# Attention: other engines for the sum of two output halves and for the scaling of probabilities

## The chip, the cores and the metric

The kernel runs on one core of a Trainium2 chip. Its metric is the device time of one execution in microseconds; lower is better. The core has a matrix engine (TensorE, in the profile PE, with its weight loads as PEld), two engines for element-wise work that can read the matrix engine's result memory PSUM (VectorE, DVE, and ScalarE, ACT), a third one without access to PSUM (GpSimd, POOL), and DMA queues (SP is one of the engines that start them). Each engine carries out its own instructions in order; between engines, semaphores order them.

## The reference, cut to what matters

Two layers of a decoder trunk: 512 tokens, 1024 features. Each layer mixes tokens in three parallel ways (sparse attention, gated linear attention, spatial gating), projects their joined outputs back, and adds a SwiGLU block. The change lies in the sparse attention, 8 heads of 64 in two groups that share keys and values. Each head has three branches, whose outputs are weighted by gates and added:

```python
s = jnp.einsum('bqghd,bcgd->bghqc', qb, kc)          # compressed keys
p_cmp = masked_softmax(s, ...)
o_cmp = jnp.einsum('bghqc,bcgd->bqghd', p_cmp, vc)
...                                                  # selected and window keys alike:
p = masked_softmax(s, tok <= t[None, None, None, :, None])
o_slc = jnp.einsum('bghqm,bgqmd->bqghd', p, vsel)
...
return gb[..., 0:1] * o_cmp + gb[..., 1:2] * o_slc + gb[..., 2:3] * o_win
```

With 512 tokens, 8 blocks of 64 and a window of 512, the selected and the window branch both become causal attention over all earlier tokens, with keys and values of their own.

## The kernel before, in words

Products run in float32 with a rounded high part and a remainder: every operand is split into `hi` (a copy into the type that TensorE rounds to) and `lo` (operand minus `hi`), and three products are added (`mm3`, L335). `split_psum` (L298) is that split: ScalarE copies `hi`, VectorE subtracts `lo`.

The attention (L1188 to L1290) goes over four pairs of heads `hp`, in each over two heads `hh`, in each over two branches `br`, in each over four tiles `i` of 128 query tokens. Tile `i` sees 128 x (i + 1) keys, so the probability tiles are 128, 256, 384 and 512 columns wide. Per branch:

- Scores: two matmuls into a bank of ring `s` (three banks), the negated row maximum on VectorE (L1218, L1237), the exponential with its row sum on ScalarE (L1222, L1239). The two narrow tiles of both branches are made together in the first branch.
- `rr`, four columns: reciprocal of the row sums and multiplication by the gate, both on VectorE (L1244, L1245).
- Scaling of the four probability tiles in place by their columns of `rr` (L1247 to L1253). `ISP` and `ISA` (L54, L55) say which tile goes where: tile 3 (512 columns) to GpSimd (L1249), tile 2 (384) to ScalarE (L1251), tiles 0 and 1 (128 and 256) to VectorE (L1253). A dependency written by hand (L1255) makes GpSimd's scaling wait for VectorE's last one.
- Transposes on TensorE (L1262) in three groups: key block 0 of all four query tiles, key block 1 of three, blocks 2 and 3 together. Each group is split by `split_psum` into `pt` (in the profile PT), and two matmuls per block, with `hi` (L1275) and `lo` (L1276), add it to the head's output bank `O`. Ring `o` has one bank only, so the next head's first L1275 needs it free.

At the head's end the compressed branch is added (L1286, L1287). `O` then holds the output in two halves, from the high and the low part of v, on different partitions. They are added into a half of `oc`, a tile of a ring of six (`tmp`): ScalarE copies one half (L1288), VectorE adds the other from PSUM (L1289). After both heads of a pair `split_psum` makes the two parts of the output projection's operand, `kt` (L1290).

Nothing here writes down the order of the engines' queues. A planner sorts the instructions by priority (program order, with offsets for some) and by its own estimate of when each is ready. So products of the output projection's first half, `out_proj(l, okt, 4, ...)` (L1673), which need nothing of the attention, lie among the attention's matmuls as fillers (L336 to L338), and so do the residual additions that go with them (L500). The queries of later heads are moved into place by GpSimd (`load_q`, L1186).

Of the kernel before, what the change touches and what calls it, by code (L numbers as in the profile page):

```python
# [10 lines left out]
F32 = mybir.dt.float32  # L11
# [5 lines left out]
ALU = mybir.AluOpType  # L17
AX = mybir.AxisListType

P = 128  # L20
# [7 lines left out]
H = 8  # L28
# [22 lines left out]
PREP = {(0, 0): (("q", 0), ("q", 1)), (0, 1): (("c", 0),), (0, 3): (("d", 0),), (1, 0): (("q", 2),), (2, 0): (("q", 3),), (2, 3): (("c", 1),),  # L51
        (4, 0): (("d", 1),)}
NBOTH = 2
ISP = (3,)  # L54
ISA = (2,)  # L55
PBK = {"g": 2, "s": 3, "t": 2, "o": 1}
JG = ((0,), (1,), (2, 3))
BTAGS = "ggsssgto"
# [85 lines left out]
def trunk_kernel(ctx: ExitStack, tc: tile.TileContext, a, out):  # L144
    nc = tc.nc
# [9 lines left out]
    def nm(s):  # L155
        uid[0] += 1
        return f"{s}_{uid[0]}"
# [7 lines left out]
    def psum(tag):  # L165
        taken[tag] += 1
        return banks[:, rings[tag][(taken[tag] - 1) % len(rings[tag])], :]

    def small(n, tag, bufs=4, dt=F32):
        return sm.tile([P, n], dt, tag=tag, name=nm(tag), bufs=bufs)  # L170
# [127 lines left out]
    def split_psum(hi, lo, src):  # L298
        nc.scalar.copy(hi, src)  # L299
        nc.vector.tensor_tensor(lo, src, hi.bitcast(F32), op=ALU.subtract)  # L300
# [88 lines left out]
    with tc.tile_pool(name="x0", bufs=1, reuse_waits="tile") as xp:  # L389
# [22 lines left out]
        def e_load(q, k0):  # L412
# [9 lines left out]
                          reason="first loads alone")  # L422
# [144 lines left out]
    def mixer(l, norm, xkt, eu=None):  # L567
# [65 lines left out]
        with tc.tile_pool(name=f"mx{l}", bufs=1, reuse_waits="tile") as mp:  # L633
            def tmp(n=SEQ, dt=F32):
                return mp.tile([P, SEQ], dt, tag="tmp", name=nm("tmp"), bufs=6)[:, 0:n]
# [11 lines left out]
            with tc.tile_pool(name=f"ma{l}", bufs=1, reuse_waits="tile") as ap:  # L647
# [29 lines left out]
                for lp in range(2):  # L677
                    hs = slice(64 * lp, 64 * lp + 64)
# [4 lines left out]
                for w_i in range(2):  # L683
                    pa = pos_t(w_i, l).rearrange("p (s a) -> p a s", s=2)
                    for s in range(2):
                        hi, lo = (kvR[w_i][:, :, 65 * s : 65 * s + 1, h] for h in range(2))
# [374 lines left out]
            with tc.tile_pool(name=f"mt{l}", bufs=1, reuse_waits="tile") as tp_:  # L1061
# [20 lines left out]
                for g in range(G):  # L1082
                    for b in range(2):
                        prep_k(g, b)
                    hi = km2[g][64:128].rearrange("p b (n c) -> p b n c", c=P)
# [99 lines left out]
                def load_q(h):  # L1185
                    (nc.gpsimd.tensor_copy if h > 1 else nc.scalar.copy)(qm1[h % GH][0:64], qst[h // GH][0:64, h % GH, :])  # L1186

                for hp in range(H // 2):  # L1188
                    if hp % 2 == 0:
                        okt[hp // 2] = kt_tile()  # L1190
                    kt = okt[hp // 2]
                    oc = tmp()
                    for hh in range(2):
                        h = 2 * hp + hh
                        g, h4 = h // GH, h % GH
# [5 lines left out]
                        O = psum(OT[h % len(OT)])  # L1201
                        first = True
                        for br in range(2):
# [23 lines left out]
                            ps_ = [pb[br] for pb in both]  # L1227
# [15 lines left out]
                            rr = small(NT, "rr", 4)  # L1243
                            nc.vector.reciprocal(rr, den)  # L1244
                            nc.vector.tensor_tensor(rr, rr, gates[:, :, 3 * h + 1 + br], op=ALU.mult)  # L1245
                            scaled = None
                            for i in SORD:  # L1247
                                if i in ISP:
                                    p3 = nc.gpsimd.tensor_tensor(ps_[i], ps_[i], rr[:, i : i + 1].to_broadcast([P, P * (i + 1)]), op=ALU.mult)  # L1249
                                elif i in ISA:  # L1250
                                    nc.scalar.activation(ps_[i], ps_[i], AF.Copy, scale=rr[:, i : i + 1])  # L1251
                                else:
                                    scaled = nc.vector.tensor_scalar(ps_[i], ps_[i], rr[:, i : i + 1], None, op0=ALU.mult)  # L1253

                            tc.add_manual_dep(p3.ins, scaled.ins.name, mybir.DependencyInfo(mybir.DependencyClass.Sync, mybir.DependencyReason.DATA),  # L1255
                                              reason="port")
                            for js in JG:
                                T = psum(TT[js[0]])
                                c = 0
# [24 lines left out]
                        hs = slice(64 * hh, 64 * hh + 64)  # L1284
# [1 line left out]
                        nc.tensor.matmul(O, lhs, pcT[g][0], start=False, stop=False)  # L1286
                        nc.tensor.matmul(O, lhs, pcT[g][1], start=False, stop=True)  # L1287
                        nc.scalar.copy(oc[hs, :], O[ls, :])  # L1288
                        nc.vector.tensor_tensor(oc[hs, :], oc[hs, :], O[hs, :], op=ALU.add)  # L1289
                    split_psum(kt[:, hp % 2, 0, :], kt[:, hp % 2, 1, :], oc)  # L1290
            return okt

    def out_proj(l, okt, k0, kts, nrm, tags=None):
# [375 lines left out]
    for l in range(L):  # L1669
        okt = mixer(l, norm, xkt, eu if l == 0 else None)  # L1670
        fnorm = Norm()
        with tc.tile_pool(name=f"ff{l}", bufs=1, reuse_waits="tile") as fp:
            out_proj(l, okt, 4, None, None)  # L1673
            fkt = [kt_tile() for _ in range(4)]
            out_proj(l, okt, 0, fkt, fnorm, BTAGS)
            ops = Ops(g_ffn(l), fkt, fp)
            if l < L - 1:
                norm = Norm()
                xkt = []
                ffn(l, fp, fnorm, fkt, ops, xkt, norm, g_attn(l + 1))  # L1680
            else:
                ffn(l, fp, fnorm, fkt, ops, None, None, None)
# [24 lines left out]
```

## Time and profile before

| | |
|---|---|
| median of 3 runs | 1287.74 us (1286.69 to 1287.77) |
| profiled execution | 1286.52 us, its span 1284.7 us, granted clock 0.997 |
| attention, layer 0 | some 183 to 282 us of the span |
| attention, layer 1 | some 814 to 912 us of the span |
| scalings on GpSimd (L1249) | 32, of 1.04 us each |
| second halves added by VectorE (L1289) | 16, of 0.68 to 0.69 us each |

How to read it: a line of a group gives the code line, the engine, the operation, output and inputs by the program's names with their shapes, the count, then busy time and the mean of one in ns, then the engine's idle time before them and what ended it. A line of a timeline gives start and duration in us, engine, line and operation, and in brackets the idle time before it and its releaser. Waits name who waited, for whom, the total, the count and the longest.

### The profile page before, as it was taken

The page shows a single profiled execution, that of the slowest core. Times are in us where ns is not written, and L with a number is a line of the kernel's source. Part 1 is how long each engine was busy: PE and PEld are TensorE (multiplying, and loading weights), DVE is VectorE, ACT ScalarE, POOL GpSimd, SP SyncE. Part 2 cuts the span into 40 slices and gives each one's busy share as a digit, 9 for nine tenths or more (in the row PEclk, how much of TensorE's full clock was granted, in tenths as well). Part 3 has the DMA queues.
Part 4 walks back from the last instruction along what each step waited for, and adds up shares of the span by engine and source line. Part 5 has one row for each costly group of instructions (what it writes and reads, how often), then busy time and mean ns, then how long its engine had stood idle before and what let it go on. Part 6 is the DMA issues. An engine that isn't in the chain of part 4 may idle for free. (4 is left out here: it accounts for less than half of the span.)

```text
span 1284.7 us, 18046 instructions
## 1 busy us (share of the span) xinstructions
PE 1257.3 (98%) x6678; PEld 1038.5 (81%) x6678; DVE 918.2 (71%) x1645; ACT 677.0 (53%) x1288; POOL 160.5 (12%) x157
## 2 busy tenths in 40 slices
PE   8999999999999999999999999999999999999997
PEld 7888788778888888888888877777788888888886
DVE  6767799977856775587446678998767457827775
ACT  6675367864533553354346733788544445515532
POOL 0101222122000100010301012121210001000102
PEclk9999999999999999999999999999999999999999
DMA  6451441034335885483434317210533448754811
GB/s 231 142 180 34 115 108 33 17 87 127 98 105 141 197 232 146 111 200 99 115 94 149 116 34 175 64 33 3 146 98 99 131 117 210 216 130 133 227 66 66
DMA packets 134204, 155.01 MB, mean 121 GB/s; under 512 B 9307, under 2 KB 86885, under 8 KB 134117
## 3 DMA queue, kind: packets, MB, share of 16 engines
q1 hardware_dynamic: 117392, 128.81, 33.3%
q0 software_dynamic: 10208, 20.84, 9.2%
q10 hardware_dynamic: 6516, 4.22, 1.5%
q8 instruction: 52, 0.85, 0.3%
q14 instruction: 36, 0.29, 0.1%
HBM read 149.92 MB, written 2.10 MB: 118 GB/s over the span
## 5 line engine op out<-in xcount | busy, mean ns | idle before, releaser
L318 ACT CAST hl<-raw 128x1024 fp32r<-128x1024 f32 (+3 forms) x170 | 175.2, 1035 | 226.5 <-PE banks L338 160.9
L321 DVE TENSOR_TENSOR hl<-raw,hl 128x1024 fp32r<-128x1024 f32 (+3 forms) x170 | 207.1, 1222 | 94.6 <-ACT hl L318 93.0
L336 PE MATMUL banks<-hl,kt 128*128 128x512 f32 (+2 forms) x688 | 257.9, 375 | 1.1 <-ACT hl L318 1.1
L337 PE MATMUL banks<-hl,kt 128*128 128x512 f32 (+2 forms) x688 | 256.4, 373 | 0.0
L338 PE MATMUL banks<-hl,kt 128*128 128x512 f32 (+2 forms) x688 | 256.1, 373 | 0.0
L337 PE MATMUL banks<-kt,hl 128*128 128x512 f32 x384 | 151.5, 394 | 0.0
L338 PE MATMUL banks<-kt,hl 128*128 128x512 f32 x384 | 151.1, 394 | 0.0
L336 PE MATMUL banks<-kt,hl 128*128 128x512 f32 x384 | 150.4, 394 | 0.0
L336 PEld LDWEIGHTS banks<-hl,kt 128*128 128x128 f32 x688 | 129.5, 188 | 23.6 <-ACT hl L318 1.9
L337 PEld LDWEIGHTS banks<-hl,kt 128*128 128x128 f32 x688 | 129.5, 188 | 21.8 <-DVE hl L321 0.3
L338 PEld LDWEIGHTS banks<-hl,kt 128*128 128x128 f32 x688 | 129.4, 188 | 21.7
L318 ACT CAST hl<-wx 128x1024 fp32r<-128x1024 f32 x48 | 50.5, 1052 | 79.8 <-PE banks L338 69.1
L337 PEld LDWEIGHTS banks<-kt,hl 128*128 128x128 f32 x384 | 72.2, 188 | 14.7 <-DVE kt L295 0.9
L338 PEld LDWEIGHTS banks<-kt,hl 128*128 128x128 f32 x384 | 72.3, 188 | 13.7
L336 PEld LDWEIGHTS banks<-kt,hl 128*128 128x128 f32 x384 | 72.0, 188 | 13.3 <-ACT kt L299 0.3
L321 DVE TENSOR_TENSOR hl<-wx,hl 128x1024 fp32r<-128x1024 f32 x48 | 58.7, 1224 | 18.4 <-ACT hl L318 18.2
L500 DVE TENSOR_TENSOR xT<-xT,banks 128x512 f32<-128x512 f32 x56 | 37.5, 681 | 47.6 <-PE banks L338 47.6
L337 PE MATMUL banks<-act,hl 128*128 128x512 f32 x172 | 67.0, 390 | 0.0
L338 PE MATMUL banks<-act,hl 128*128 128x512 f32 x172 | 66.9, 389 | 0.0
L336 PE MATMUL banks<-act,hl 128*128 128x512 f32 x172 | 66.9, 390 | 0.0
L300 DVE TENSOR_TENSOR PT<-banks,PT 128x384 fp32r<-128x384 f32 (+1 forms) x96 | 54.6, 597 | 14.1 <-ACT PT L299 13.2
L336 PE MATMUL banks<-hl,act 128*128 128x512 f32 (+1 forms) x164 | 63.0, 384 | 0.0
(356 smaller groups left out, 2404.1 us busy)
## 6 DMA issues: line engine op xcount, KB each, us to landing
raw<-in_w_gate_dram SPq DMA_DIRECT2D x44, 512.0 KB, 3.9
raw<-in_w_up_dram SPq DMA_DIRECT2D x44, 512.0 KB, 4.0
raw<-in_w_in_dram SPq DMA_DIRECT2D x32, 512.0 KB, 3.7
raw<-in_w_down_dram SPq DMA_DIRECT2D x36, 256.0 KB, 4.0
raw<-in_w_down_dram SPq DMA_DIRECT2D x18, 512.0 KB, 3.7
raw<-in_w_out_dram SPq DMA_DIRECT2D x16, 512.0 KB, 4.3
raw<-in_cmp_w_k_dram SPq DMA_DIRECT2D x8, 512.0 KB, 3.9
raw<-in_cmp_w_v_dram SPq DMA_DIRECT2D x8, 512.0 KB, 4.9
```

Source lines behind the costliest of these rows:

```text
L300: nc.vector.tensor_tensor(lo, src, hi.bitcast(F32), op=ALU.subtract)
L318: last_cast[:] = [nc.scalar.copy(hl[:, 0, 0:n], raw[:, 0:n])]
L321: e_.tensor_tensor(hl[:, 1, 0:n], raw[:, 0:n], hl[:, 0, 0:n].bitcast(F32), op=ALU.subtract)
L336: nc.tensor.matmul(ps, lh, rh, start=start, stop=False, skip_group_check=skip)
L337: nc.tensor.matmul(ps, lh, rl, start=False, stop=False, skip_group_check=skip)
L338: return nc.tensor.matmul(ps, ll, rh, start=False, stop=stop, skip_group_check=skip)
L500: nc.vector.tensor_tensor(xT[:, m, :], xT[:, m, :], ps, op=ALU.add)
```

## The change

Three things change. Tile 2 of the probabilities (384 columns) is scaled by GpSimd too, tile 1 (256) by ScalarE, and only tile 0 (128) by VectorE; both GpSimd scalings wait for VectorE's one. In the first three pairs of a layer the second half of a head's output is copied by ScalarE into a tile of its own, `od`, instead of being added by VectorE. For these pairs a `join` adds the halves and makes the operand's low part on GpSimd, with ScalarE's copy for the high part in between; it stands in the program behind the scaling of the next pair's first branch. The fourth pair is treated as before.

```diff
-ISP = (3,)
-ISA = (2,)
+ISP = (2, 3)
+ISA = (1,)
...
+                joins = []
+
+                def join(hi, lo, oc, od):
+                    nc.gpsimd.tensor_tensor(oc, oc, od, op=ALU.add)
+                    nc.scalar.copy(hi, oc)
+                    nc.gpsimd.tensor_tensor(lo, oc, hi.bitcast(F32), op=ALU.subtract)
+
...
                     oc = tmp()
+                    od = tmp() if hp < H // 2 - 1 else oc
...
-                            scaled = None
+                            scaled, p3s = None, []
                             for i in SORD:
                                 if i in ISP:
-                                    p3 = nc.gpsimd.tensor_tensor(ps_[i], ps_[i], rr[:, i : i + 1].to_broadcast([P, P * (i + 1)]), op=ALU.mult)
+                                    p3s.append(nc.gpsimd.tensor_tensor(ps_[i], ps_[i], rr[:, i : i + 1].to_broadcast([P, P * (i + 1)]), op=ALU.mult))
...
-                            tc.add_manual_dep(p3.ins, scaled.ins.name, mybir.DependencyInfo(mybir.DependencyClass.Sync, mybir.DependencyReason.DATA),
-                                              reason="port")
+                            for p3 in p3s:
+                                tc.add_manual_dep(p3.ins, scaled.ins.name, mybir.DependencyInfo(mybir.DependencyClass.Sync, mybir.DependencyReason.DATA),
+                                                  reason="port")
+                            if joins:
+                                join(*joins.pop())
...
                         nc.scalar.copy(oc[hs, :], O[ls, :])
-                        nc.vector.tensor_tensor(oc[hs, :], oc[hs, :], O[hs, :], op=ALU.add)
-                    split_psum(kt[:, hp % 2, 0, :], kt[:, hp % 2, 1, :], oc)
+                        if od is oc:
+                            nc.vector.tensor_tensor(oc[hs, :], oc[hs, :], O[hs, :], op=ALU.add)
+                        else:
+                            nc.scalar.copy(od[hs, :], O[hs, :])
+                    if od is oc:
+                        split_psum(kt[:, hp % 2, 0, :], kt[:, hp % 2, 1, :], oc)
+                    else:
+                        joins.append((kt[:, hp % 2, 0, :], kt[:, hp % 2, 1, :], oc, od))
```

## The prediction

> **What bounds the kernel now.** I read the page first, then the table by stage, then the waits of TensorE's weight loads, which show what each loaded column block had to wait for.
>
> ```profile
> span 1284.7 us, 18046 instructions
> ...
> PE 1257.3 (98%) x6678; PEld 1038.5 (81%) x6678; DVE 918.2 (71%) x1645; ACT 677.0 (53%) x1288; POOL 160.5 (12%) x157
> ```
>
> TensorE has work in 98% of the span. No other engine can be worth more than the moments in which TensorE stands still, so the question is how many of these lie in the stage that the change touches. The table by stage has, per row, the stretch, its length, and the busy time with the number of instructions for PE, PEld, DVE, ACT and POOL. The two rows are the first and the second half of layer 0's attention.
>
> ```profile
> 183.00:232.00 49.00, 47.03 (x269) 38.13 (x268) 46.16 (x107) 38.62 (x106) 10.74 (x12) 1.00 0.09 28
> 232.00:282.00 50.00, 46.62 (x259) 35.82 (x257) 39.83 (x91) 36.37 (x101) 10.76 (x10) 1.00 0.26 63
> ```
>
> In the first half VectorE is busy 46.16 of 49 us, ScalarE 38.62, GpSimd (POOL) 10.74. TensorE still reaches 47.03, since the planner fills its gaps with products of the output projection. In the second half TensorE loses 3.4 us. So the stage is short of VectorE time and has much POOL time left. The waits of layer 0 (175 to 290 us; who waited for whom, total us, times, longest):
>
> ```profile
> PEld banks L1275 <- ACT PT L299: 7.6, 18, 1.2
> PEld banks L1276 <- DVE PT L300: 3.7, 10, 0.9
> PEld banks L1262 <- POOL P L1249: 2.6, 6, 0.8
> ```
> ```profile
> PE banks L1275 <- DVE tmp L1289: 0.8, 1, 0.8
> ```
>
> Three links of one chain stop TensorE: POOL's scaling holds the transposes (L1262), ScalarE's high part of the transposed probabilities (PT) holds the first product with v, VectorE's low part the second. The evacuation of the head's output bank (L1289) does so once. Layer 1 is the same chain again, so I price one layer and double it.
>
> **The change part by part.** The durations, from one profiled execution (count, then busy time and mean ns; for the lines asked for alone, min/median/max ns):
>
> ```profile
> L1239 ACT ACTIVATE P<-banks,nmx 128x512 f32<-128x512 f32 x16 | 11.2, 700 | 3.0 <-DVE nmx L1237 3.0
> L1251 ACT ACTIVATE P<-P,rr 128x384 f32<-128x384 f32 x16 | 10.0, 624 | 4.1 <-DVE rr L1245 4.1
> ...
> L1239 ACT ACTIVATE P<-banks,nmx 128x384 f32<-128x384 f32 x16 | 9.4, 589 | 2.3 <-PE banks L1262 1.7 <-DVE nmx L1237 0.3 <-DVE PT L300 0.2
> ...
> L1288 ACT COPY tmp<-banks 64x512 f32<-64x512 f32 x8 | 4.7, 581 | 3.4 <-PE banks L1287 3.3
> ...
> L299 ACT CAST kt<-tmp 128x512 fp32r<-128x512 f32 x4 | 2.5, 625 | 0.8 <-DVE tmp L1289 0.8
> ```
> ```profile
> L1253 DVE TENSOR_SCALAR P<-P,rr 128x256 f32<-128x256 f32 x16 | 5.6, 347 | 0.0
> L1289 DVE TENSOR_TENSOR tmp<-tmp,banks 64x512 f32<-64x512 f32 x8 | 5.5, 684 | 3.3 <-ACT tmp L1288 3.0
> ...
> L1253 DVE TENSOR_SCALAR P<-P,rr 128x128 f32<-128x128 f32 x16 | 4.5, 279 | 0.1
> L1245 DVE TENSOR_TENSOR rr<-rr,gates 128x4 f32<-128x4 f32 x16 | 4.3, 268 | 0.1
> ...
> L300 DVE TENSOR_TENSOR kt<-tmp,kt 128x512 fp32r<-128x512 f32 x4 | 2.8, 688 | 0.7 <-ACT kt L299 0.7
> ```
> ```profile
> L1249 POOL TENSOR_TENSOR P<-P,rr x32: 1039/1040/1043, 183.3 to 902.0; 128x512 f32<-128x512 f32 x32
> ```
> ```profile
> L1383 POOL TENSOR_TENSOR yg<-zb,gf x6: 1281/1292/1297, 1252.7 to 1270.3; 128x512 f32<-128x512 f32 x6
> ```
> ```profile
> L905 POOL TENSOR_TENSOR kr<-tmp,tmp x8: 721/736/1050, 124.5 to 776.0; 128x256 f32<-128x256 f32 x8
> ```
>
> *Work per layer.* VectorE loses 16 scalings of 256 columns (16 x 0.347 = 5.6), the additions of six heads (6 x 0.684 = 4.1) and the low parts of three pairs (3 x 0.688 = 2.1): 11.8 us, none added. ScalarE scales 256 instead of 384 columns; 128 columns are worth 0.700 - 0.589 = 0.11, so 0.51 for 0.62, 16 x 0.11 = 1.8 less; six second copies of an output half add 6 x 0.58 = 3.5; net +1.7. The three copies of the pair's high part (0.625) stay, at a later place. POOL gets 16 scalings of 384 columns and three joins. The 384 is not in the trace: its bounds are the 0.72 of a 256 addition and the 1.04 of 512. Additions of two full tiles cost 1.28 at 512 and 0.72 at 256, 2.2 ns a column; the 512 scaling with its repeated factor costs 1.04, so I scale 1.28 - 128 x 0.0022 = 1.00 by 1.04/1.28 and take 0.81, nearer to the 512 row, which is the same instruction. A join is two operations on two full 512 tiles, 2 x 1.28 = 2.6. POOL gains 16 x 0.81 + 3 x 2.6 = 20.8 us a layer and would stand at about 42 of 99: no bound by its sum, only by its delays.
>
> *The POOL link.* POOL starts after VectorE's last scaling and now has two in a row. Head 7 of layer 0:
>
> ```profile
> 269.10 0.55 DVE L1253 TENSOR_SCALAR P<-P,rr 128x128 f32<-128x128 f32 x2
> ...
> 269.81 1.04 POOL L1249 TENSOR_TENSOR P<-P,rr 128x512 f32<-128x512 f32 x1 [7.55 <-ACT P L1239]
> 269.98 0.89 DVE L1245 TENSOR_TENSOR rr<-rr,gates 128x4 f32<-128x4 f32 x1
> ...
> 270.91 0.66 PE L1262 MATMUL banks<-ident,P 128*128 128x128 f32 x4 [0.20 <-POOL P L1249]
> ...
> 270.97 0.61 ACT L1251 ACTIVATE P<-P,rr 128x384 f32<-128x384 f32 x1 [1.23 <-DVE rr L1245]
> ```
>
> The two VectorE scalings took 0.55 together, the first 0.28, so POOL may start 0.26 earlier; its 0.81 more makes the 512 tile ready 0.55 later, and TensorE's transpose, which today starts 0.06 after POOL's end (269.81 + 1.04 = 270.85, then 270.91), moves with it. Six of a layer's sixteen scalings stop TensorE (the wait row above). They are of two kinds; head 4 shows the other:
>
> ```profile
> 240.36 0.68 DVE L300 TENSOR_TENSOR kt<-tmp,kt 128x512 fp32r<-128x512 f32 x1
> 240.96 0.28 DVE L1253 TENSOR_SCALAR P<-P,rr 128x128 f32<-128x128 f32 x1
> 241.29 0.56 DVE L300 TENSOR_TENSOR PT<-banks,PT 128x384 fp32r<-128x384 f32 x1
> 241.76 0.34 DVE L1253 TENSOR_SCALAR P<-P,rr 128x256 f32<-128x256 f32 x1
> ```
> ```profile
> 242.27 1.04 POOL L1249 TENSOR_TENSOR P<-P,rr 128x512 f32<-128x512 f32 x1 [5.53 <-DVE P L1253]
> ```
>
> Here something lay between the two scalings, so dropping the second pays for the 384 by itself (241.24 + 0.17 + 0.81 + 1.04 = 243.26 against 243.31; 0.17 is the time from VectorE's end to POOL's start here). Besides, the pair's low part at 240.36 goes away and the chain starts 0.6 sooner. Counting three of each kind: 3 x 0.55 = +1.65 and -0.6 per layer. The other ten scalings end before TensorE asks; what hides their delay is earlier work in TensorE's queue.
>
> *What waits behind POOL.* The multiplication of four columns, all 32 of it:
>
> ```profile
> L1245 DVE TENSOR_TENSOR rr<-rr,gates x32: 93/160/892, 181.9 to 900.4; 128x4 f32<-128x4 f32 x32
> ```
>
> At 269.98 it took 0.89 instead of the median's 0.16, and ended with POOL's instruction; the mean of 268 ns above says that it isn't alone. ScalarE, which runs in order, then waited 1.23 for it. With POOL occupied for 1.85 instead of 1.04 this lasts up to 0.81 longer, at some four heads a layer; mostly the same moment as the late transpose, so I add 0.5 a layer (bounds 0 and 4 x 0.81 = 3.2).
>
> [...]
>
> *The output bank.* Today ScalarE copies one half and VectorE adds the other. Head 5 (VectorE, then ScalarE):
>
> ```profile
> 261.09 0.69 DVE L1289 TENSOR_TENSOR tmp<-tmp,banks 64x512 f32<-64x512 f32 x1
> 261.81 1.16 DVE L300 TENSOR_TENSOR PT<-banks,PT 128x512 fp32r<-128x512 f32 x2
> ```
> ```profile
> 260.92 0.97 ACT L299 CAST PT<-banks 128x512 fp32r<-128x512 f32 x2
> ```
>
> The addition ends at 261.78 and the low part follows at once. Two ScalarE copies in a row instead push the high part back by about 0.5 (0.58 less the overlap of two neighbours), while the low part need not queue: +0.2 and -0.4 per layer. In heads 0 to 3 fillers cover either; heads 6 and 7 keep the addition.
>
> *The joins.* Those of heads 2 and 4 fit into POOL's idle time (5.53 above). Head 6's doesn't:
>
> ```profile
> 261.23 1.04 POOL L1249 TENSOR_TENSOR P<-P,rr 128x512 f32<-128x512 f32 x1 [0.78 <-PE banks L1262]
> ```
> ```profile
> 263.46 0.71 PE L1262 MATMUL banks<-ident,P 128*128 128x128 f32 x5
> ```
>
> POOL is idle for 0.78 between the head's two branches, and the second branch's widest tile is needed at about 263.9, 1.6 after its end at 262.27. A first join operation (1.28) just fits ahead of the second branch; if the other half gets in between too, 1.0 is lost. I take half: +0.5 (bounds 0 and 1.0).
>
> *The sum.* 1.65 - 0.6 + 0.5 + 0.2 - 0.4 + 0.5 = +1.85 a layer, +3.7 in all. From the profiled execution's 1286.5 that is 1290.2; the median of the runs (1287.74) stands 1.2 above that execution, so 1291.4.
>
> **The rivals.**
> *VectorE's relief decides (faster).* VectorE was busy 86.0 of these 99 us and loses 11.8. If half of the waits for low parts (1.9), the wait for the output bank (0.8) and, through earlier maxima and exponentials, a third of the waits for high parts (2.5) go, 5.2 a layer are won against costs of 1.65 + 0.5 + 0.2 = 2.35: -2.85 a layer, 1286.5 - 5.7 + 1.2 = 1282.0; without the costs 1277.3. For it speaks the first half's 46.16 of 49. Against it: the largest wait is ScalarE's, which gets more work, and on head 7's path the removed pieces lie only just ahead of POOL. It decides if the planner, with less VectorE work, leaves fillers over for the second half.
> *Nothing shows.* The planner lays the order anew from its own estimates; it can put a filler or the next head's scores where POOL is late. Gains and losses of 1 to 2 us a layer then cancel: 1287.7.
> *POOL in VectorE's way.* If each of four multiplications waits the whole 0.81 and head 6's join costs its 1.0, the layer's sum is 1.85 - 0.5 + 3.2 + 0.5 = 5.05: 1286.5 + 10.1 + 1.2 = 1297.8. It decides once POOL passes from one instruction to the next without letting VectorE in.
>
> **How the numbers follow.** About 0.2% (2.6 us) is what a measurement of this kernel can tell from no change. The forecast, 1291.4, gets 0.34; POOL in VectorE's way 0.09; nothing shows 0.22; VectorE's relief 0.35. So faster 0.35, same 0.22, slower 0.43. Both signs hold much of the chance, so the range spans them, from 1279.5, between the relief's two prices, to 1297.0, just short of the collision's; the forecast's own range goes from 1288.9, the lower bounds of its terms (3 x 0.46 with the 384 at 0.72, then -0.6 + 0.2 - 0.4), to 1294.6, half of the way to the collision.
>
> **What would show it.** Right: the last transposes of heads 5 to 7 start about 0.5 later after VectorE's first scaling and end their idle time on POOL more often than six times a layer; the four-column multiplication's mean goes above 268 ns; ScalarE's busy time in these stretches stays near 75 us while VectorE's falls from 86 to about 74; TensorE's busy time in the second half falls below 46.6 of 50. Wrong: VectorE's low-part waits shrink below 2 us a layer and TensorE's idle time with them, or the POOL waits stay at 2.6.

## The result, and the profile after

The change makes the kernel slower: 1304.7 us (1304.13 to 1306.28, 4 runs) against 1287.76 for the kernel before, run beside it, a ratio of 1.0134 with a 95% interval of 1.0116 to 1.0152. The side was forecast, the size was not: 17 us instead of 3.7, beyond the range's upper end of 1297.0.

The page of the changed kernel's profile, whose execution took 1304.13 us:

```profile
span 1302.3 us, 18064 instructions
...
PE 1262.9 (97%) x6678; PEld 1041.2 (80%) x6678; DVE 900.7 (69%) x1595; ACT 680.7 (52%) x1300; POOL 204.9 (16%) x201
```

VectorE has 17.5 us less to do than before, GpSimd 44.4 more, ScalarE 3.7 more. The span grows by 17.6. The table by stage over layer 0's attention, which now runs to about 290 (stretch, length, busy time of PE, PEld, DVE, ACT, POOL, then the granted clock):

```profile
183.00:232.00 49.00, 45.07 (x254) 35.72 (x254) 40.60 (x92) 36.20 (x99) 19.05 (x20) 1.00 0.09 28
232.00:290.00 58.00, 50.83 (x274) 39.19 (x274) 36.26 (x81) 41.14 (x111) 23.88 (x24) 0.97 0.20 49
```

VectorE fell from 46.16 to 40.60 us in the first half, as intended, and TensorE fell with it, from 47.03 to 45.07: no gain from the relief shows here. In the second half TensorE is idle for 7.2 of 58 us, where it was 3.4 of 50. There is also a new number in the clock's column, 0.97. What the weight loads waited for, layer 0 (175 to 300 us):

```profile
PEld banks L1273 <- POOL P L1257: 8.6, 15, 1.2
PEld banks L1286 <- ACT PT L299: 6.3, 16, 1.4
PEld banks L336 <- ACT kt L1192: 3.3, 2, 2.1
PEld banks L1287 <- DVE PT L300: 1.6, 5, 0.6
PEld banks L1286 <- ACT tmp L1303: 1.2, 2, 0.7
```

Lines moved: L1273 is the transpose, L1257 GpSimd's scaling, L1286 and L1287 the products with the high and the low part, L1192 ScalarE's copy in the join, L1303 the second copy of the output bank. Set against before: waits for VectorE's low parts more than halved, 3.7 to 1.6; waits for ScalarE's high parts are a little down, 7.6 to 6.3; waits for GpSimd's scaling more than tripled, from 6 occasions and 2.6 us to 15 and 8.6 (seven pairs and one, in 8 of the layer's 16 branches: where TensorE waits it now mostly does so twice, once for the 384 tile and once for the 512 one); and two waits are new, a product of the output projection (L336) behind the join, and the output bank behind its second copy.

The durations of the new operations, from the groups by shape:

```profile
L1257 POOL TENSOR_TENSOR P<-P,rr 128x512 f32<-128x512 f32 x32 | 35.2, 1100 | 0.0
...
L1257 POOL TENSOR_TENSOR P<-P,rr 128x384 f32<-128x384 f32 x32 | 27.1, 846 | 102.3 <-DVE P L1261 55.9 <-PE banks L1273 17.2 <-ACT tmp L1146 11.4
...
L1193 POOL TENSOR_TENSOR kt<-tmp,kt 128x512 fp32r<-128x512 f32 x6 | 7.7, 1276 | 4.4 <-ACT kt L1192 4.4
L1191 POOL TENSOR_TENSOR tmp<-tmp,tmp 128x512 f32<-128x512 f32 x6 | 7.6, 1271 | 0.0
```

So the prices were right: 0.85 us for the scaling of 384 columns (0.81 estimated), 1.27 to 1.28 for each half of a join (1.28). Only the 512 scaling rose, from 1040 to 1100 ns on the mean. What was wrong is what they hold up. The place in head 6 of layer 0 that the prediction had picked out, in order of time:

```profile
268.80 1.82 POOL L1257 TENSOR_TENSOR P<-P,rr 128x384 f32<-128x384 f32 x2 [2.54 <-DVE P L1261]
...
269.73 0.50 PE L1286 MATMUL banks<-PT,vst 128*128 128x512 f32 x1 [0.24 <-ACT tmp L1303]
...
270.59 1.26 POOL L1191 TENSOR_TENSOR tmp<-tmp,tmp 128x512 f32<-128x512 f32 x1
271.88 0.62 ACT L1192 CAST kt<-tmp 128x512 fp32r<-128x512 f32 x1 [1.32 <-POOL tmp L1191]
272.40 0.51 ACT L1259 ACTIVATE P<-P,rr 128x256 f32<-128x256 f32 x1
...
272.55 0.50 PE L336 MATMUL banks<-kt,hl 128*128 128x512 f32 x1 [1.88 <-ACT kt L1192]
272.58 1.28 POOL L1193 TENSOR_TENSOR kt<-tmp,kt 128x512 fp32r<-128x512 f32 x1 [0.73 <-ACT kt L1192]
```

GpSimd finishes both scalings at 270.6 and only then adds the halves. ScalarE has the copy of that sum next in its queue and stands for 1.32 us, with the scaling of the 256 tile behind it, which the head's transposes need. TensorE has a filler product that reads the copy next in its queue and stands for 1.88. TensorE's transposes of this branch come at 273.07 only, so nobody had to wait for the scalings here: the prediction had looked at GpSimd's queue alone.

### The profile page after: what moved, and what is told of

It reads as the page before. It is cut to its first block, busy times and chain, and to the rows that moved or that the text cites. A ratio compares the mean times of both kernels' runs of the same rounds, so it can differ in the third digit from the quotient of the medians.

```text
span 1302.3 us, 18064 instructions
## 1 busy us (share of the span) xinstructions
PE 1262.9 (97%) x6678; PEld 1041.2 (80%) x6678; DVE 900.7 (69%) x1595; ACT 680.7 (52%) x1300; POOL 204.9 (16%) x201
## 4 chain that ended last, share of the span: by engine, by line
PE 77%; DVE 8%; ACT 7%; POOL 4%; issue 3%; DMA 2%; ACTq 0%; POOLq 0%; DVEq 0%
PE banks L336 21%; PE banks L337 21%; PE banks L338 21%; POOL P L1257 3%; PE banks L1273 2%; ACT hl L318 1%; DMA raw<-in_w_in_dram 1%; PE banks L1286 1%; PE banks L1287 1%; DVE hl L321 1%; PE banks L1616 1%; PE banks L471 1%; PE banks L969 1%; ACT PT L299 1%; DVE w1h L743 1%
## 5 line engine op out<-in xcount | busy, mean ns | idle before, releaser
L336 PE MATMUL banks<-hl,kt 128*128 128x512 f32 (+2 forms) x688 | 257.9, 375 | 1.1 <-ACT hl L318 1.1
L336 PE MATMUL banks<-kt,hl 128*128 128x512 f32 x384 | 151.9, 397 | 5.4 <-ACT kt L1192 5.4
L336 PEld LDWEIGHTS banks<-hl,kt 128*128 128x128 f32 x688 | 129.5, 188 | 23.6 <-ACT hl L318 2.0
L336 PEld LDWEIGHTS banks<-kt,hl 128*128 128x128 f32 x384 | 72.3, 189 | 20.1 <-ACT kt L1192 6.6
L338 PEld LDWEIGHTS banks<-kt,hl 128*128 128x128 f32 x384 | 72.3, 188 | 13.5
L1257 POOL TENSOR_TENSOR P<-P,rr 128x384 f32<-128x384 f32 x64 | 61.0, 973 | 102.3 <-DVE P L1261 55.9
L1273 PE MATMUL banks<-ident,P 128*128 128x128 f32 x320 | 58.9, 287 | 9.1 <-POOL P L1257 7.6
L337 PE MATMUL banks<-act,hl 128*128 128x512 f32 x172 | 67.0, 390 | 0.0
L338 PE MATMUL banks<-act,hl 128*128 128x512 f32 x172 | 66.9, 389 | 0.0
```

The lines of the kernel that those rows point to most:

```text
L336: nc.tensor.matmul(ps, lh, rh, start=start, stop=False, skip_group_check=skip)
L337: nc.tensor.matmul(ps, lh, rl, start=False, stop=False, skip_group_check=skip)
L338: return nc.tensor.matmul(ps, ll, rh, start=False, stop=stop, skip_group_check=skip)
L1257: p3s.append(nc.gpsimd.tensor_tensor(ps_[i], ps_[i], rr[:, i : i + 1].to_broadcast([P, P * (i + 1)]), op=ALU.mult))
L1273: nc.tensor.transpose(T[:, c : c + P], ps_[i][:, j * P : (j + 1) * P], ident)
```

## The experiments

All ratios are against the kernel before, run beside it on the same chip, with 95% intervals; what was expected is quoted as it was on record before the run.

**The two halves of the change.** The new split without joins (`od = oc` for every pair, so nothing is deferred), and the joins with the old split (`ISP = (3,)`, `ISA = (2,)`):

```diff
-                    od = tmp() if hp < H // 2 - 1 else oc
+                    od = oc
```

> Only the new split of the scalings; the halves of the outputs are added by VectorE as before. Theory A (GpSimd's second scaling in a row makes TensorE's transposes wait in almost every branch): 1297 to 1301 us, some 10 to 13 above before, and the transposes' waits for GpSimd in layer 0 stay at 8 us or more (2.6 before, 8.6 after). Rival B (the joins make the loss): within 3 us of before.

> Only the joins; the scalings as before. Theory A: 1292 to 1295 us, because a filler product and ScalarE's later work stand behind the join's ScalarE copy, some 3 us a layer. Rival B: 1300 us or more.

Measured: 1.0043 (1.0028 to 1.0058), 1292.1 us, for the split; 1.0071 (1.0056 to 1.0086), 1295.7 us, for the joins. Their product, 1.0114, lies just under the whole change's interval. So both lose, the joins more: neither theory had the proportion right. The split alone already has the transposes' waits (both layers, 5.3 us and 12 occasions before):

```profile
PEld banks L1273 <- POOL P L1257: 16.9, 25, 1.7
```

**GpSimd's delay by itself.** Kernel before, with one more multiplication in GpSimd's queue ahead of the scaling:

```diff
-                                    p3 = nc.gpsimd.tensor_tensor(ps_[i], ps_[i], ...)
+                                    d_ = nc.gpsimd.tensor_tensor(scr, scr, rr[:, 2:3].to_broadcast([P, 384]), op=ALU.mult)
+                                    with tc.issue_after(d_.ins):
                                         p3 = nc.gpsimd.tensor_tensor(ps_[i], ps_[i], ...)
...
-                            tc.add_manual_dep(p3.ins, scaled.ins.name, ...)
+                            for p_3 in (d_, p3):
+                                tc.add_manual_dep(p_3.ins, scaled.ins.name, ...)
```

> The kernel before, with one more GpSimd multiplication of 384 columns on a tile that nobody reads, ahead of each scaling of the 512 tile: VectorE and ScalarE keep all their work, GpSimd's result comes 0.83 us later. Theory A: at least as slow as the new split alone, 12 to 16 us above before. Rival C (the new loads of VectorE and ScalarE change the planner's order, and that costs): at most 4 us above before.

Measured: 1.0119 (1.0099 to 1.014). 0.85 us more in each of 32 branches, 27 us of delay, cost 15. Theory A holds: nothing was taken from or given to VectorE and ScalarE, and the kernel loses nearly as much as by the whole change. Not all of it need be the wait itself: the four runs go from 1299.29 us at a granted clock of 0.997 to 1304.06 at 0.994. And the loss isn't read off the waits. TensorE's transposes wait 12.8 us for GpSimd here (12 times, both layers), less than the 16.9 us (25 times) of the split, which lost 5.5. The two kernels also differ in the load of VectorE and ScalarE and in the planner's order, so neither loss gives a price for a delay.

**The delay the other way.** Kernel before; half of the widest tile stays unscaled:

```diff
-p3 = nc.gpsimd.tensor_tensor(ps_[i], ps_[i], rr[:, i : i + 1].to_broadcast([P, P * (i + 1)]), op=ALU.mult)
+p3 = nc.gpsimd.tensor_tensor(ps_[i][:, 0:256], ps_[i][:, 0:256], rr[:, i : i + 1].to_broadcast([P, 256]), op=ALU.mult)
```

> The kernel before, with only 256 of the 512 columns of the widest tile scaled, so GpSimd's link is some 0.45 us shorter and nothing else changes. Theory A (GpSimd's link is in the chain in most branches): 3 to 8 us faster than before. Rival I (today's order covers the link, only its lengthening shows): within 3 us of before.

Measured: 0.9975 (0.9966 to 0.9984), 3.2 us less, on the border between theory A and rival I. GpSimd's link is in the chain of the kernel before too, though a shortening pays much less than a lengthening costs.

**VectorE's relief by itself.** Kernel before with work left out on VectorE alone:

```diff
-                                else:
+                                elif i == 0:
                                     scaled = nc.vector.tensor_scalar(ps_[i], ps_[i], rr[:, i : i + 1], None, op0=ALU.mult)
...
-                        nc.vector.tensor_tensor(oc[hs, :], oc[hs, :], O[hs, :], op=ALU.add)
+                        if hp == H // 2 - 1:
+                            nc.vector.tensor_tensor(oc[hs, :], oc[hs, :], O[hs, :], op=ALU.add)
```

> The kernel before with work left out: the 256 tiles stay unscaled and in the first three pairs the second half of a head's output isn't added, so VectorE loses 9.7 us a layer and no engine gets anything. Theory G (VectorE's load isn't what holds the chain): within 3 us of before. Rival H (the relief is worth what the prediction's rival priced, 5.2 us a layer, and the change only hides it under its costs): 1276 to 1280 us.

Measured: 1.0003 (0.9994 to 1.0013). The waits of its layer 0 show that the relief arrived:

```profile
PEld banks L1275 <- ACT PT L299: 7.1, 19, 1.2
PEld banks L1262 <- POOL P L1249: 2.3, 4, 0.8
PEld banks L1276 <- DVE PT L300: 2.2, 8, 0.5
```

The low-part waits went from 3.7 to 2.2 and the time did not move. The edit also lets GpSimd start after VectorE's scaling of 128 columns, since that one is now the last, and even with this help nothing was won. Rival H falls: an engine that was busy for 46 of 49 us was not what held the kernel.

**ScalarE in place of GpSimd or VectorE.** Two moves of scalings without joins. `ISP = (3,)`, `ISA = (1, 2)`:

> The scalings of 256 and of 384 columns both on ScalarE, the 512 one on GpSimd as before, no joins: VectorE is relieved as in the change, GpSimd isn't loaded. Theory A: no loss, 1283 to 1289 us. Rival C (ScalarE is what holds the chain, and every us added to it shows): 3 to 10 us above before, as it gets 8 us a layer more.

Measured: 1.0056 (1.0039 to 1.0073). And, in the kernel before, the two wide tiles exchanged, `ISP = (2,)`, `ISA = (3,)`:

> The kernel before with the two wide tiles exchanged: GpSimd scales 384 columns (0.83 instead of 1.04 us), ScalarE 512 (some 0.73 instead of 0.62). Theory A: 1 to 4 us faster than before. Rival C (what ScalarE gets shows at once): 1 to 4 us slower.

Measured: 1.0048 (1.0033 to 1.0063). Theory A fails in both. Rival C has the right sign in both: the kernel loses when ScalarE gets more, even where GpSimd's link gets 0.2 us shorter. In the exchange it loses 6 us and not 1 to 4, although ScalarE gets only some 3.4 us in 32 branches (729 instead of 624 ns each), so something else is in it. ScalarE is in the chain three times per branch (exponential, scaling, high part).

**The wait written by hand.** The split alone, without GpSimd's wait for VectorE's scaling; no data need that wait, since each tile is scaled by one engine:

```diff
-                            for p3 in p3s:
-                                tc.add_manual_dep(p3.ins, scaled.ins.name, mybir.DependencyInfo(...), reason="port")
```

> The new split of the scalings without joins, and without GpSimd's wait for VectorE's scaling: the data need none. Theory A: GpSimd starts 0.3 to 0.4 us earlier in each branch and some half of the 6 us that the split alone costs is gone, 1288 to 1290 us. [...]

Measured: 0.9984 (0.9975 to 0.9994), 1285.45 us: better than theory A's, and the fastest kernel here that does all of the work, a little ahead of the kernel before. TensorE's waits for GpSimd's scaling, 16.9 us in the split, are down to

```profile
PEld banks L1270 <- POOL P L1257: 5.2, 11, 1.0
PEld banks L1270 <- DVE P L1261: 4.4, 6, 1.2
```

and the second row, waits for VectorE's scaling, is new. The groups show the price that the wait had avoided on VectorE's scaling of 128 columns, first in the split with the wait, then here:

```profile
L1261 DVE TENSOR_SCALAR P<-P,rr 128x128 f32<-128x128 f32 x32 | 9.0, 281 | 0.4
```
```profile
L1261 DVE TENSOR_SCALAR P<-P,rr 128x128 f32<-128x128 f32 x32 | 17.7, 554 | 0.4
```

That is 0.27 us a branch on VectorE, which can afford it, against an earlier start of two GpSimd operations in a row. The same edit in the kernel before and in the whole change:

> The kernel before without that wait. Theory A: GpSimd starts some 0.5 us earlier, 1281 to 1285 us. Rival J (GpSimd and VectorE's scalings hold each other up): 1287 to 1291.

> The whole change without GpSimd's wait for VectorE's scaling. Theory A (the split's loss is the longer GpSimd link, the joins' loss is their own): the joins' 9 us or so stay, 1294 to 1299 us. Rival K (the joins lose only by lengthening the same link): 1290 us or less.

Measured: before without the wait 1.0007 (0.9998 to 1.0016), so there it is worth nothing, and rival J has the time (VectorE's scalings took 462 and 467 ns instead of 279 and 347); the whole change without it 1.0107 (1.0092 to 1.0122), 1301.4 us. Theory A had hoped for at most 1299; the joins lose even more beside the free split, 1.0107 against 0.9984, than by themselves. TensorE's clock is hardly the reason: one execution of this kernel had a granted clock of 0.998 (the profiled kernel before: 0.997) and took 1301.20 us. The wait of the filler product is still there, 6.0 us in both layers.

**What the joins are made of.** One part at a time, all with the old split. The second ScalarE copy alone (VectorE adds from there at once, split in its old place):

> Only the second ScalarE copy: VectorE adds the halves from there at once and the split stands where it was. Rival E (the copy is what the joins lose by): 3 to 6 us above before, with waits of the first product with v for that copy. Theory L (GpSimd's addition and the product that waits for it are the rest): at most 2 above before.

Measured: 1.0028 (1.0016 to 1.0039), 3.6 us, as rival E had it. TensorE's waits for the high part, which now queues behind two copies, grew from 3.2 us and 8 occasions (both layers) to

```profile
PE banks L1285 <- ACT PT L299: 5.4, 10, 1.2
```

The later place alone, split by ScalarE and VectorE:

> Only the later place: VectorE adds from PSUM as before, and the split by ScalarE and VectorE stands behind the scaling of the next pair's first branch. Theory L: within 2 us of before. If it is 3 or more above, the later place by itself makes the planner's order worse.

Measured: 1.0003 (0.9993 to 1.0012): free. The later place with the low part on GpSimd, halves added by VectorE from PSUM:

> VectorE adds the halves as before; only the split is deferred, high part on ScalarE and low part on GpSimd. Theory D: one hop only and nothing waits for GpSimd but a product of the projection, within 3 us of before. Rival E: within 3 us of before as well, since the second copy is gone. If it is over 5 us above before, the place of the split and not the hops or the copy is what costs.

Measured: 1.0013 (1.0004 to 1.0022). Copy and later place together, addition and low part on VectorE (`gpsimd` replaced by `vector` in `join`):

> Joins alone, with addition and low part on VectorE instead of GpSimd; the second ScalarE copy and the later place stay. Theory D: the hop is short, at most 3 us above before. Rival E: still 6 us or more above before.

Measured: 1.0026 (1.0017 to 1.0036), no more than the copy alone. So of the joins' 0.71%, some 0.28 is the copy, 0.13 the low part on GpSimd, nothing the later place; some 0.3 comes only with GpSimd's addition ahead of the split, if the parts simply add up (each interval is some 0.1 wide to either side). Three edits tried to say by what. High part on GpSimd too (`nc.gpsimd.tensor_copy(hi, oc)`); join behind the second branch (`if joins and br == 1:`); addition written where nobody reads it (`tensor_tensor(od, oc, od, ...)`), the last also in the whole change:

> Joins alone, with the high part copied by GpSimd too, so that nothing of ScalarE waits for GpSimd. Theory D (the two hops GpSimd, ScalarE, GpSimd stand in the way of what is queued behind them on ScalarE and of the filler product that reads the high part): about half of the 9.8 us that the joins alone cost are gone, 1289 to 1292 us. Rival E (the second ScalarE copy of the output bank is what costs): no change, 1294 to 1297. Rival F (TensorE stands long enough to lose its clock, whatever the join's engine): dips of the clock stay and 1293 to 1297.

> Joins alone, placed behind the scaling of the next pair's second branch instead of its first. Theory D: the filler product stands later in TensorE's queue and the wait for the join's ScalarE copy shrinks, 1288 to 1293 us. Rival E: 1294 to 1297, as the second copy is where it was.

> Joins alone, with GpSimd's addition written where nobody reads it: the high and low parts are made of the first half only, so the second half is missing from the output. All instructions stay, ScalarE's copy no longer waits for GpSimd's addition. Theory M (what the joins lose beside the second copy is that wait, ScalarE and a filler product standing behind it): 1289 to 1292 us, as with the join on VectorE. Rival N (GpSimd's additional time holds up the scalings): 1294 to 1297, as with the joins alone.

> The whole change with GpSimd's addition written where nobody reads it, the second half missing from the output as before. Theory M: the split's 6 and the copy's 4 us stay, 1296 to 1299 us. Rival N: 1301 us or more, since the scalings still queue behind the joins.

Measured: 1.0111 (1.009 to 1.0132), 1.0061 (1.0046 to 1.0076), 1.0103 (1.0076 to 1.0129) and 1.009 (1.007 to 1.0109). Theory D expected the first to win half of the loss back, and it lost more; the clock stayed low, 0.990 to 0.993, as rival F had said, but the time lies above that rival's too. The later place took most of the filler product's wait away (3.8 to 0.6 us in both layers) and the loss stayed within the interval, as rival E had it.

Taking away ScalarE's wait for the addition has two answers. In the joins alone it won nothing: two of the four runs, at a clock of 0.997, took 1297.18 and 1298.39 us, about what the joins cost with the wait, and two at 0.993 took 1302.33 and 1303.45. In the whole change it won about a third of the loss, 1.009 instead of 1.0134, with intervals that don't touch, and its 1299.2 us lies at the edge of theory M's range and below rival N's. So theory M falls for the joins alone and is nearly right in the whole change. The weight loads of the joins alone, both layers, show a wait that only moved on to the next operation of the join:

```profile
PEld banks L336 <- ACT kt L1192: 4.2, 4, 1.8
...
PEld banks L337 <- POOL kt L1193: 3.9, 3, 1.9
```

In layer 0's last join the first product that reads the copy starts at 266.77 us instead of 269.42, and the next one then stands 1.62 us for GpSimd's low part. That the planner placed them earlier because the copy was due earlier is the likely reason, not a shown one.

## Why the prediction was wrong

- **The failing step is the joins.** "Those of heads 2 and 4 fit into POOL's idle time", "I take half: +0.5" a layer, and with "+0.2 and -0.4" for the copy: about nothing. Alone they cost 0.71%, 9 us. The working asked whether GpSimd had room, and not who reads the result: ScalarE's queue and, through the fillers, TensorE's (272.55 above). The copy was priced at 0.2 a layer for one head; done alone it cost 0.28%, about 1.8 a layer, six heads together.
- **The split's size was nearly right, its account incomplete.** Its terms (1.65 and the 0.5 for what waits behind GpSimd) made 4.3 us, and 0.43% is 5.5. In layer 0 of the changed kernel GpSimd stops TensorE in 8 of 16 branches, where six were counted, but in seven of them twice. The working followed the 512 tile alone; the 384 tile, which ScalarE had scaled before, now comes from GpSimd too, and TensorE waits for it first (transposes at 184.09, when GpSimd's 384 scaling ends, and again at 185.09, when its 512 scaling ends). And the loss hangs on the hand-written wait, which the working took as given: without it the split is no slower than before (0.9984).
- **The 0.5 for POOL in VectorE's way had the wrong mechanism.** The four-column multiplication, which was to go above 268 ns, fell to 170 on the mean, and its longest from 892 to 340. The rival built on it fails with it. VectorE does lose time beside GpSimd, but elsewhere: its 256-column scaling took 411 ns on the mean instead of 347 with the joins alone, and its 128-column one 554 instead of 281 in the split without the wait.
- **The rival of VectorE's relief**, given 0.35, fails. The run that left VectorE's work out lowered its busy time by 13.5 us (918.2 to 904.7), about three quarters of the change's 17.5, and gave 1.0003.
- **The terms that spoke for the change** (-0.6 for the pair's low part, -0.4 for the queue behind the addition) were VectorE's time too, and nothing in the runs supports them: with only the pair's low part moved to GpSimd, at the later place, the kernel lost 0.13%.
- **Not in the working at all: TensorE's clock.** In the changed kernel three stretches inside the attention run at half clock, one in layer 0 and two in layer 1 (last section). If TensorE was what held the kernel in them, half of 3 x 3.41 us, 5.1 at most, is theirs. The four runs speak against so much: their clocks were 0.993, 0.993, 0.995 and 0.996, with 0.997 for the profiled kernel before, and the one at 0.996 still took 1304.64 us. No run took the clock away alone, so the share stays open.

Open is why GpSimd's addition ahead of the split costs some 0.3% by itself and more beside the free split. In the joins alone it isn't one wait: taking away ScalarE's, or the filler's, left the loss. In the whole change taking away ScalarE's won about 0.4%; why there and not here is open too. A candidate that no run tested by itself: in the joins alone GpSimd's addition of layer 0's first join runs from 216.05 us for 1.27, and beside it VectorE's scaling of 256 columns takes 1.3 to 1.4 us instead of 0.35. GpSimd's 512 scaling, which waits for VectorE by hand, starts only at 217.64. VectorE's longest scaling took 1.39 to 1.41 us in all four runs of the joins alone with GpSimd's addition, and at most 0.35 in those without. No run held the planner's order fixed.

## What to carry to other kernels

How busy an engine is doesn't say what its relief is worth: leave its work out for one run and look. Before work goes to an idle engine, ask who stands behind its result in the queues of the other engines, fillers included, and price the whole chain from the last input to the first reader. A hand-written wait should be tried again whenever the operation behind it grows: here it was neutral for one GpSimd operation and cost 0.6% for two (0.3% in the whole change).

## What the runs showed of the hardware

In this kernel TensorE lost half of its clock after stretches in which it was busy for part of the time. The windows of the changed kernel ahead of the half clock, at it, and the other two at half clock (clock in the third column from the end):

```profile
243.59:247.00 3.41, 1.50 (x7) 0.74 (x6) 2.44 (x4) 2.63 (x7) 2.68 (x4) 1.00 0.00 0
247.00:250.41 3.41, 3.41 (x13) 2.87 (x12) 0.92 (x2) 2.48 (x8) 0.93 (x1) 0.50 0.00 0
```
```profile
885.29:888.70 3.41, 3.41 (x11) 2.77 (x12) 0.56 (x1) 2.51 (x10) 1.25 (x1) 0.50 0.00 0
912.60:916.01 3.41, 3.41 (x14) 3.03 (x13) 1.85 (x5) 2.15 (x7) 0.14 (x1) 0.50 0.02 5
```

A stretch of 3.41 us in which seven matmuls ran, 1.50 us of busy time (44%), is followed by one of the same length at 0.50; the stretches ahead of the other two, 881.88 to 885.29 and 909.19 to 912.60, were busy for 1.71 and 1.53 us. In the kernel before, the clock stayed at 1.00 after a stretch with more work:

```profile
857.97:861.38 3.41, 2.61 (x13) 1.48 (x12) 3.32 (x10) 3.18 (x9) 2.08 (x2) 1.00 0.00 0
861.38:864.79 3.41, 3.37 (x22) 2.69 (x21) 3.41 (x9) 2.76 (x10) 0.00 (x0) 1.00 0.08 20
```

Busy time alone doesn't draw the line, though. In the changed kernel the stretch from 270.89 to 274.30 us was busy for 1.75 us and the next had 1.00, while with the joins alone the one from 848.99 to 852.40 was busy for 2.59 us and the next had 0.50. What else counts, these runs don't show.

The wait between GpSimd's scalings and VectorE's has a price on either side. In the split, leaving it out raised VectorE's 128-column scaling from 281 to 554 ns and GpSimd's 384-column one from 899 to 955, while GpSimd's 512-column one fell from 1163 to 1056; the kernel with the wait was slower by 0.6%. So in this kernel the longer operations cost less than the later start that the wait brings; by what the two hold each other up, these runs don't show.

In both profiles VectorE and ScalarE read PSUM (L1289, 0.68 us, and L1288, 0.58, before), while none of GpSimd's 157 and 201 instructions reads or writes it; whether it could, no run tried.
